# A hybrid decoder block on one core: the later modulation rows in half blocks, and the next chunk's squares one per step

## The chip, the cores and the metric

The kernel runs on one core of one Trainium2 chip. The metric is the device time of one execution in microseconds (us). Before the change it is 2672.51 us, the median of 3 runs (2671.59 to 2675.07). PE is the matmul engine, PEld its weight load, DVE the vector engine, ACT the scalar engine, POOL the GpSimd engine, and SP the engine whose queue issues every DMA of this kernel.

## The reference

The input is a residual stream of 2048 positions by 1024 channels, a condition vector c, and the weights of one decoder layer, all float32.

```
mod = silu(c) @ w_ada + b_ada                # 6 x 1024: sh1, sc1, g1, sh2, sc2, g2
h = rms_norm(x, norm1_g) * (1 + sc1) + sh1
proj = h @ w_in                              # gq gk gv gr glr | aq ak av
y = concat(gla_group(...), dilated_attention_group(...))
x = x + g1 * (y @ w_out)
h = rms_norm(x, norm2_g) * (1 + sc2) + sh2
u = causal_depthwise_conv(h @ w_up, conv_w, conv_b)
out = x + g2 * ((silu(u_gate) * u_val) @ w_down)
```

The modulation vector `mod` has 48 columns of 128 values here. Columns 0 to 15 (sh1, sc1) are wanted before the first projection. Columns 16 to 47 (g1, sh2, sc2, g2), the later modulation, are wanted only when the projections of all chunks are through and the output projection begins.

## The kernel before, in words

**Tiling.** Positions are worked in four chunks of 512 (`T`), channels in blocks of 128 partitions. A float32 product is made of three matmuls in fp32r (`mm3`, L288 to L290): high weights with high input, and the two cross terms. So each block of weights of 512 KB is loaded (`wraw`, 2 slots), rounded on ACT (`whi`, L226, 3 slots) and its remainder taken on DVE (`wlo`, L227, 3 slots), and the matmuls wait for both. `weights` asks for blocks two ahead of their use, in the order of `plan`.

**Stages.** `run` first makes sh1 and sc1 and the normalised input of chunk 0. Then come the projections of the four chunks (`proj`, 26 steps each, a generator that yields after each step), the mixers (`mix`: gated linear attention, then four pairs of attention heads), and per chunk `outproj` and `ffn`. Generators are woven together: `beside` and `along` advance one generator by so many steps for so many steps of the other. The first 27 steps of the projections run alone, the rest beside `mix(0)`, and each later mixer beside the feed-forward part of the chunk before.

**What sets the order.** The program text only gives each instruction a priority. A scheduler at build time puts the instructions of each engine in a fixed list, by priority and by what it believes to be ready, and gives out the slots of tagged tiles. On the chip each engine works through its list in order, and so does SP with the DMAs: an instruction that waits holds up all that stands behind it in its list. The build alone tells the order, and it is shown below with line numbers of the kernel it belongs to.

**The later modulation.** For column b, `ada(b)` loads a 128x1024 row block of `w_ada` (512 KB) into a tile `wada`, yields, and then multiplies it by the condition and sums along the row in one DVE instruction (L330, the product; a second tiny instruction reads the sum), adds the bias (L331), and for sc2 makes the gain `G2` (L335). The 32 later columns share one slot (tag `v4`, also used by the attention's `v4` tile), so the load of column b+1 waits for the product of column b. The generator of the 32 columns is advanced 32 steps for each 46 steps of the projections. The first of these loads (b = 16) waits for a product near the end of the start (`gate_ins`).

**The next chunk's statistics.** `norm_stats(src(c))` loads the eight 128x512 blocks of the chunk's input (256 KB each, tile `sq`, 3 slots), squares each on ACT into another `sq` tile (L360), and sums them on DVE into `acc` (tile `rstd`, 2 slots; L363 copies the first, L365 adds the others). One matmul with `ones` (L367) averages over channels, and Ln and Exp (L369, L370) give the factor. `ahead(proj(c - 1), 10, c)` calls it in one piece after ten steps of the projection before. The blocks are loaded again later for the normalised input (`begin`, through `norm_mod1`, L380 to L384).

Of the kernel before, what the change touches and what calls it, by code (L numbers as in the profile page):

```python
# [19 lines left out]
P = 128  # L20
T = 512
NCH = 4
KD = 8
# [86 lines left out]


def along(a, na, b, nb):

    acc = 0.0
    done = object()
    for _ in b:
        acc += na / nb
        while acc >= 1.0:
            acc -= 1.0
            if next(a, done) is done:  # L120
                acc = -1e9
        yield
    for _ in a:
        pass


def chain(*gs):
    for g in gs:
        yield from g


class K:
# [181 lines left out]

        self.tc.add_manual_dep(inst.ins, self.gate_ins.ins.name, mybir.DependencyInfo(mybir.DependencyClass.Sync, mybir.DependencyReason.DATA))

    def ada(self, b, raws=None):

        nc = self.nc
        if raws is None:  # L320
            raws = [self.at.tile([P, 1024], F32, name="wada", tag="v4", bufs=1)]
        n = 1024 // len(raws)
        for i, raw in enumerate(raws):
            ld = nc.sync.dma_start(raw, self.A["w_ada"][b][:, i * n:(i + 1) * n])
            if b == 16:
                self.after(ld)
        yield
        m = self.mod[:, b:b + 1]
        for i, raw in enumerate(raws):
            self.last = nc.vector.tensor_tensor_reduce(raw, raw, self.cond[:, i * n:(i + 1) * n], 0.5, m if i else 0.0, ALU.mult, ALU.add, m)  # L330
        nc.vector.tensor_tensor(m, m, self.ba[:, b:b + 1], op=ALU.add)  # L331
        for j, G, g in ((1, self.G1, self.n1), (4, self.G2, self.n2)):
            if b // KD == j:
                k = b % KD
                nc.vector.scalar_tensor_tensor(G[:, k:k + 1], m, 1.0, g[:, k:k + 1], op0=ALU.add, op1=ALU.mult)  # L335


    def load_x(self, c):
# [14 lines left out]

    def norm_stats(self, src):

        nc = self.nc
        acc = None
        for k in range(KD):
            sq = self.tmp.tile([P, T], F32, name="sq", bufs=3)
            nc.scalar.activation(sq, src(k), AF.Square)  # L360
            if acc is None:
                acc = self.tmp.tile([P, T], F32, name="rstd", bufs=2)
                nc.vector.tensor_copy(acc, sq)  # L363
            else:
                nc.vector.tensor_tensor(acc, acc, sq, op=ALU.add)  # L365
# [575 lines left out]
    def run(self):  # L941
        self.ada_setup()
        self.scratch()
        self.x1, self.h2, self.tail = {}, {}, ()
        xs = self.load_x(0)
        rstd = {0: self.norm_stats(lambda k: xs[k])}
        h0, ws, done = [], {}, {b: self.pg() for b in FIRST}
        spare = self.at.tile([P, 2048], F32R, name="w0", tag="kt", bufs=2)
        ring = self.at.tile([P, 2048], F32, name="ring", tag="kt", bufs=2)
        for k in range(KD):  # L950
            big = [self.at.tile([P, 1024], F32, name="wada", tag="big", bufs=4)]
            pair = [self.gp.tile([P, T], F32, name="wada", tag=t) for t in ("ghi", "glo")] if k < 5 else [ring[:, k % 2 * 1024:k % 2 * 1024 + 1024]]
            gs = [self.ada(KD + k, big), self.ada(k, pair)]
            for g in gs:
                next(g)
            if k < len(FIRST):
                b = FIRST[k]
                ws[b] = self.wblock(self.A["w_ch"][b], KD, P, True, spare if k == 3 else None)
            for g in gs:
                next(g, None)  # L960
            if k == GATE:
                self.gate_ins = self.last
            h0.append(self.norm_mod1(xs[k], k, rstd[0], self.G1, self.mod[:, 0:8]))
        for b in FIRST:
# [12 lines left out]

        self.wleft, self.wready, self.wpos = list(self.plan()), [], 0
        hs = [h0]

        def begin(c):
            hs.append(self.norm_mod(src(c), rstd[c], self.G1, self.mod[:, 0:8]))

        def proj(c):
            yield from self.proj(c, hs.pop(), (lambda: begin(c + 1)) if c < 3 else None, () if c else done)

        def ahead(g, n, c):

# [12 lines left out]
        for _ in chain(self.outproj(3), self.ffn(3)):  # L1001
            pass
# [61 lines left out]
```

## Time and profile before

| | us |
|---|---|
| median of 3 runs (lowest, highest) | 2672.51 (2671.59, 2675.07) |
| profiled execution: its time, its span | 2676.88, 2675.1 |
| PE busy | 2595.0 (97%) |
| PE weight load busy | 2122.1 (79%) |
| DVE busy | 1891.1 (71%) |
| ACT busy | 1273.2 (48%) |
| POOL busy | 512.1 (19%) |
| mean granted PE clock | 0.989 of full speed |

The span runs from the first to the last instruction of the program. The busy time of PE includes overlap of pipelined matmuls, so what is left of the span is a rough measure of its idle time. DMA moved 405 MB at a mean of 151 GB/s. Times inside the profile are counted from the start of the span. A row of a timeline gives start, duration, engine, line, operation, tiles and count, and in brackets the idle time of the engine before it and what ended that idle time. A row of a wait list gives who waited for whom, the total in us, how often, and the longest.

### The profile page before, as it was taken

The page shows a single profiled execution, that of the slowest core. Times are in us where ns is not written, and L with a number is a line of the kernel's source. Part 1 is how long each engine was busy: PE and PEld are TensorE (multiplying, and loading weights), DVE is VectorE, ACT ScalarE, POOL GpSimd, SP SyncE. Part 2 cuts the span into 40 slices and gives each one's busy share as a digit, 9 for nine tenths or more (in the row PEclk, how much of TensorE's full clock was granted, in tenths as well). Part 3 has the DMA queues.
Part 4 walks back from the last instruction along what each step waited for, and adds up shares of the span by engine and source line. Part 5 has one row for each costly group of instructions (what it writes and reads, how often), then busy time and mean ns, then how long its engine had stood idle before and what let it go on. Part 6 is the DMA issues. An engine that isn't in the chain of part 4 may idle for free.

```text
span 2675.1 us, 46823 instructions
## 1 busy us (share of the span) xinstructions
PE 2595.0 (97%) x18152; PEld 2122.1 (79%) x18152; DVE 1891.1 (71%) x3756; ACT 1273.2 (48%) x2607; POOL 512.1 (19%) x308
## 2 busy tenths in 40 slices
PE   5988999999989999999999999999999999999999
PEld 3777878888768888888788788878888888788887
DVE  8676784665676866777887777778777766666665
ACT  3445556656645455443545444445455443433332
POOL 1142451212221311101231111022211110111110
PEclk9999999999989999999999999999999999999999
DMA  7868455554552244447434444643344445323222
GB/s 276 295 212 276 160 173 170 186 188 150 173 175 95 93 126 133 124 125 241 135 100 135 133 133 129 197 156 122 104 141 138 140 132 180 131 95 101 97 95 95
DMA packets 192127, 405.09 MB, mean 151 GB/s; under 512 B 19473, under 2 KB 70434, under 8 KB 190626
## 3 DMA queue, kind: packets, MB, share of 16 engines
q1 hardware_dynamic: 191906, 402.11, 46.0%
q8 instruction: 143, 2.34, 0.4%
q14 instruction: 78, 0.64, 0.1%
HBM read 339.12 MB, written 62.91 MB: 150 GB/s over the span
## 4 chain that ended last, share of the span: by engine, by line
PE 77%; DVE 5%; ACT 3%; DMA 2%; issue 1%; POOL 0%; SPq 0%; DVEq 0%; ACTq 0%; POOLq 0%
PE psg L288 22%; PE psg L289 22%; PE psg L290 22%; PE psa L719 2%; PE psa L699 2%; PE psa L821 2%; PE psa L557 1%; DVE wlo L227 1%; ACT whi L226 1%; PE psa L816 1%; PE psa L735 1%; ACT big L709 1%; PE psa L627 0%; PE psa L628 0%; DMA sq<-y 0%
## 5 line engine op out<-in xcount | busy, mean ns | idle before, releaser
L288 PE MATMUL psg<-hhi,whi 128*128 128x512 f32 x2040 | 808.7, 399 | 15.6 <-ACT hhi L382 9.0
L289 PE MATMUL psg<-hlo,whi 128*128 128x512 f32 x2040 | 805.6, 395 | 6.4 <-DVE hlo L384 5.0
L290 PE MATMUL psg<-hhi,wlo 128*128 128x512 f32 x2040 | 803.9, 395 | 0.0
L226 ACT CAST whi<-wraw 128x1024 fp32r<-128x1024 f32 (+1 forms) x391 | 409.6, 1049 | 402.5 <-PE psg L289 307.5
L227 DVE TENSOR_TENSOR wlo<-wraw,whi 128x1024 fp32r<-128x1024 f32 (+1 forms) x300 | 386.1, 1287 | 150.2 <-ACT whi L226 141.4
L227 POOL TENSOR_TENSOR wlo<-wraw,whi 128x1024 fp32r<-128x1024 f32 x91 | 223.7, 2459 | 1340.8 <-ACT whi L226 1138.9
L288 PEld LDWEIGHTS psg<-hhi,whi 128*128 128x128 f32 x2040 | 386.2, 190 | 104.8 <-ACT hhi L382 12.3
L289 PEld LDWEIGHTS psg<-hlo,whi 128*128 128x128 f32 x2040 | 386.4, 189 | 90.3 <-DVE hlo L384 9.8
L290 PEld LDWEIGHTS psg<-hhi,wlo 128*128 128x128 f32 x2040 | 386.5, 189 | 82.3 <-issue 2.0
L288 PE MATMUL psg<-ghi,whi 128*128 128x512 f32 x704 | 280.1, 398 | 0.0
L289 PE MATMUL psg<-glo,whi 128*128 128x512 f32 x704 | 277.1, 394 | 0.0
L290 PE MATMUL psg<-ghi,wlo 128*128 128x512 f32 x704 | 276.3, 392 | 0.0
L933 DVE SCALAR_TENSOR_TENSOR x<-psg,mod,x 128x512 f32<-128x512 f32 x192 | 142.7, 747 | 124.4 <-PE psg L290 120.2
L889 DVE SCALAR_TENSOR_TENSOR y<-psg,conv_w_sb,y 128x511 f32<-128x511 f32 x176 | 130.9, 744 | 88.2 <-ACT y L888 87.9
L288 PE MATMUL psg<-whi,hhi 128*128 128x512 f32 (+2 forms) x512 | 177.5, 353 | 10.5 <-DVE stg L461 7.0
L289 PE MATMUL psg<-wlo,hhi 128*128 128x512 f32 (+2 forms) x512 | 178.7, 349 | 7.2 <-DVE wlo L227 7.2
L290 PE MATMUL psg<-whi,hlo 128*128 128x512 f32 (+2 forms) x512 | 177.3, 349 | 0.0
L288 PEld LDWEIGHTS psg<-ghi,whi 128*128 128x128 f32 x704 | 132.5, 188 | 32.2 <-issue 4.5
L290 PEld LDWEIGHTS psg<-ghi,wlo 128*128 128x128 f32 x704 | 132.5, 188 | 28.4 <-issue 1.0
L289 PEld LDWEIGHTS psg<-glo,whi 128*128 128x128 f32 x704 | 132.7, 188 | 28.1 <-issue 2.1
L709 ACT ACTIVATE big<-big,nm 128x256 f32<-128x256 f32 (+1 forms) x256 | 122.4, 479 | 47.1 <-DVE nm L724 47.1
L581 POOL TENSOR_TENSOR pt<-kt,pt 128x512 f32<-128x512 f32 x56 | 92.4, 1650 | 264.2 <-ACT pt L578 186.5
(199 smaller groups left out, 3617.7 us busy)
## 6 DMA issues: line engine op xcount, KB each, us to landing
wraw<-in_w_up_dram SPq DMA_DIRECT2D x176, 512.0 KB, 3.3
wraw<-in_w_down_dram SPq DMA_DIRECT2D x88, 512.0 KB, 3.3
wraw<-in_w_ch_dram SPq DMA_DIRECT2D x48, 512.0 KB, 4.2
wada<-in_w_ada_dram SPq DMA_DIRECT2D x40, 512.0 KB, 5.0
v<-v SPq DMA_DIRECT2D x68, 256.0 KB, 5.1
wraw<-in_w_tokw_dram SPq DMA_DIRECT2D x32, 512.0 KB, 3.9
wraw<-in_w_out_dram SPq DMA_DIRECT2D x32, 512.0 KB, 4.0
sq<-in_xT_dram SPq DMA_DIRECT2D x48, 256.0 KB, 3.9
```

The costliest lines, as they stand in the source:

```text
L226: nc.scalar.copy(hi[:, :n], raw[:, :n])
L227: (nc.gpsimd if pool else nc.vector).tensor_tensor(lo[:, :n], raw[:, :n], hi[:, :n].bitcast(F32), op=ALU.subtract)
L288: nc.tensor.matmul(ps, wh, hh, start=first and k == 0, stop=False, skip_group_check=shared)
L289: nc.tensor.matmul(ps, wh, hl, start=False, stop=False, skip_group_check=shared)
L290: nc.tensor.matmul(ps, wl, hh, start=False, stop=k == n - 1, skip_group_check=shared)
L581: nc.gpsimd.tensor_tensor(kh, gk, df, op=ALU.mult)
L699: nc.tensor.matmul(at(i, hh, z), q[H[hh], i * P:(i + 1) * P], key(H[hh], i, z), start=True, stop=True, skip_group_check=True)
L709: nc.scalar.activation(t[:, lo:hi], t[:, lo:hi], AF.Exp, bias=nm[:, hh, g, i:i + 1], scale=2.0 ** -(h + 1), accum_out=dn[:, hh, g, i:i + 1])
L719: nc.tensor.transpose(ps[:n, i * P:(i + 1) * P], part(S[hh], i), self.C("id"))
L821: nc.tensor.matmul(out, lhsT, rhs, start=first[hh], stop=False, skip_group_check=True)
L889: nc.vector.scalar_tensor_tensor(y[:, 1:], ps[:, :T - 1], self.cw[:, 1, b:b + 1], y[:, 1:], op0=ALU.mult, op1=ALU.add)
L933: nc.vector.scalar_tensor_tensor(x1, ps, self.mod[:, 40 + cb:41 + cb], x1, op0=ALU.mult, op1=ALU.add)
```

## The change

- The later modulation is loaded and multiplied in half blocks: 64 loads of 128x512 (256 KB) and 64 products, in a slot of their own (tag `th`, one slot, otherwise used by the feed-forward part only). A column's second product adds to the sum of its first. The load is traced one step ahead of its product, so the load of a half block waits for the product of the half block before.
- The generator of the 64 half blocks is advanced 64 steps for each 98 steps of the projections, of which there are 104 (before: 32 steps for each 46).
- The statistics of the next chunk are a generator too (`stats`): one load, one square and one addition per step, the load a step ahead; ten steps are spread over the first 16 steps of the projection before. The square is written over its own input, so a block holds one `sq` slot and not two.

```diff
-    def ada(self, b, raws=None):
+    def ada(self, b, raws):
...
+    def ada_late(self):
+
+        nc = self.nc
+        for i in (2, 4, 3, 5):
+            for b in range(8 * i, 8 * i + KD):
+                m = self.mod[:, b:b + 1]
+                for j in range(2):
+                    cols = slice(j * T, (j + 1) * T)
+                    raw = self.up.tile([P, T], F32, name="wada", tag="th", bufs=1)
+                    ld = nc.sync.dma_start(raw, self.A["w_ada"][b][:, cols])
+                    if b == 16 and not j:
+                        self.after(ld)
+                    yield
+                    nc.vector.tensor_tensor_reduce(raw, raw, self.cond[:, cols], 0.5, m if j else 0.0, ALU.mult, ALU.add, m)
+                self.ada_end(b)
...
+    def square(self, acc, x, sq=None):
+
+        nc = self.nc
+        if sq is None:
             sq = self.tmp.tile([P, T], F32, name="sq", bufs=3)
...
+        nc.scalar.activation(sq, x, AF.Square)
+        if acc is None:
+            acc = self.tmp.tile([P, T], F32, name="rstd", bufs=2)
+            nc.vector.tensor_copy(acc, sq)
+        else:
+            nc.vector.tensor_tensor(acc, acc, sq, op=ALU.add)
+        return acc
...
-        def ahead(g, n, c):
-
-            for i, _ in enumerate(g):
-                if i == n:
-                    rstd[c] = self.norm_stats(src(c))
+        def stats(c):
+
+            acc = None
+            x = src(c)(0)
+            for k in range(KD):
                 yield
-
-        gemm = along(chain(*(self.ada(8 * i + k) for i in (2, 4, 3, 5) for k in range(KD))), 32, chain(ahead(proj(0), 10, 1), ahead(proj(1), 10, 2), ahead(proj(2), 10, 3), proj(3)), 46)
+                nx = src(c)(k + 1) if k + 1 < KD else None
+                acc = self.square(acc, x, x)
+                x = nx
+            yield
+            rstd[c] = self.norm_end(acc)
+            yield
+
+        def ahead(c):
+
+            return along(stats(c), 10, proj(c - 1), 16)
+
+        gemm = along(self.ada_late(), 64, chain(ahead(1), ahead(2), ahead(3), proj(3)), 98)
```

`ada_end` holds the bias and gain instructions of `ada` unchanged, and `norm_end` the matmul, Ln and Exp of `norm_stats`. The rows below are the order in which the build puts the instructions: line, operation, output and inputs with tile numbers, size. The line numbers of the changed kernel are its own: L351 is the late product (L330 before), L347 its load, L332 and L336 bias and gain, L383 the square, L386 and L388 copy and addition, L999 the load of an input block, L464 the copy of a finished projection out of PSUM (L437 before), L447 the scaling of a query or key (L420 before), L367 and L369 the two DVE steps of its Newton iteration (L350 and L352 before).

**First place: the start of the late products on DVE.** `wada_496` is the first later block, `wlo_511` (before) and `wlo_517` (now) the remainder of the same first block of `w_av0` weights that the first matmuls after the start wait for.

```order
L330 ISA wada_496,mod_109<-wada_496,cond_93 128x1024
L330 ISA mod_109 128x1
L331 TENSOR_TENSOR mod_109<-mod_109,b_ada_sb_99 128x1
L363 COPY rstd_865<-sq_861 128x512
L227 TENSOR_TENSOR wlo_511<-wraw_508,whi_510 128x1088
L330 ISA wada_503,mod_109<-wada_503,cond_93 128x1024
```

Now:

```order
L386 COPY rstd_509<-sq_496 128x512
L351 ISA wada_498,mod_109<-wada_498,cond_93 128x512
L351 ISA mod_109 128x1
L388 TENSOR_TENSOR rstd_509<-rstd_509,sq_506 128x512
L388 TENSOR_TENSOR rstd_509<-rstd_509,sq_589 128x512
L351 ISA wada_512,mod_109<-wada_512,cond_93,mod_109 128x512
L351 ISA mod_109 128x1
L227 TENSOR_TENSOR wlo_517<-wraw_514,whi_516 128x1088
```

Ahead of the first weights' remainder stand two half products with a load between them, where one whole product stood, and three steps of the statistics where one stood.

On ACT at the same place, `whi` is the rounded first block and `stg_490` the copy that empties the first PSUM bank:

```order
L360 ACTIVATE sq_861<-sq_862 128x512
L226 CAST whi_510<-wraw_508 128x1088
L437 ACTIVATE stg_490<-psg_210 128x512
L360 ACTIVATE sq_867<-sq_868 128x512
L226 CAST whi_516<-wraw_514 128x1088
```

Now:

```order
L383 ACTIVATE sq_496<-sq_496 128x512
L383 ACTIVATE sq_506<-sq_506 128x512
L383 ACTIVATE sq_589<-sq_589 128x512
L226 CAST whi_516<-wraw_514 128x1088
L383 ACTIVATE sq_680<-sq_680 128x512
L464 ACTIVATE stg_490<-psg_210 128x512
```

Four squares stand ahead of the copy where one stood; the fourth, of `sq_680`, needs the slot of `sq_496`, which the first copy on DVE sets free.

**Second place: DVE in the last key blocks of chunk 0.** `stg_1331` (before) and `stg_1309` (now) are the same scaled key block, which ACT waits for (`o16`, L430 before).

```order
L330 ISA wada_1756,mod_109<-wada_1756,cond_93 128x1024
L330 ISA mod_109 128x1
L350 SCALAR_TENSOR_TENSOR nwt_1339<-psa_1334,eps_103,sq_1325 128x512
L331 TENSOR_TENSOR mod_109<-mod_109,b_ada_sb_99 128x1
L352 SCALAR_TENSOR_TENSOR sq_1325<-nwt_1339,sq_1325 128x512
L330 ISA wada_1790,mod_109<-wada_1790,cond_93 128x1024
L330 ISA mod_109 128x1
L420 SCALAR_TENSOR_TENSOR stg_1331<-stg_1332,kgs_473,sq_1325 128x512
```

Now:

```order
L351 ISA wada_2661,mod_109<-wada_2661,cond_93 128x512
L351 ISA mod_109 128x1
L367 SCALAR_TENSOR_TENSOR nwt_1317<-psa_1312,eps_103,sq_1303 128x512
L369 SCALAR_TENSOR_TENSOR sq_1303<-nwt_1317,sq_1303 128x512
L351 ISA wada_2723,mod_109<-wada_2723,cond_93,mod_109 128x512
L351 ISA mod_109 128x1
L447 SCALAR_TENSOR_TENSOR stg_1309<-stg_1310,kgs_473,sq_1303 128x512
```

The two products around the Newton steps keep their places and are of half the width.

**Third place: DVE in the query blocks of chunk 1**, where before all later products are done. `wlo_2481` and `wlo_2561` (before) are the same weights as `wlo_2472` and `wlo_2509` (now).

```order
L227 TENSOR_TENSOR wlo_2481<-wraw_2478,whi_2480 128x1024
L352 SCALAR_TENSOR_TENSOR sq_2202<-nwt_2217,sq_2202 128x512
L420 SCALAR_TENSOR_TENSOR stg_2208<-stg_2209,qgs_471,sq_2202 128x512
L227 TENSOR_TENSOR wlo_2561<-wraw_2558,whi_2560 128x1024
L566 COPY_PREDICATED kt_1792<-masks_sb_460,psa_2332 128x128
```

Now:

```order
L227 TENSOR_TENSOR wlo_2472<-wraw_2469,whi_2471 128x1024
L332 TENSOR_TENSOR mod_109<-mod_109,b_ada_sb_99 128x1
L369 SCALAR_TENSOR_TENSOR sq_2189<-nwt_2204,sq_2189 128x512
L351 ISA wada_4847,mod_109<-wada_4847,cond_93 128x512
L351 ISA mod_109 128x1
L447 SCALAR_TENSOR_TENSOR stg_2195<-stg_2196,qgs_471,sq_2189 128x512
L227 TENSOR_TENSOR wlo_2509<-wraw_2506,whi_2508 128x1024
L351 ISA wada_5031,mod_109<-wada_5031,cond_93,mod_109 128x512
```

Here a half product now stands about every third instruction. In the whole list the last late product stands, before, ahead of the 31st weights' remainder of DVE, and now between the 42nd and the 43rd, which is in the last key blocks of chunk 1. On PE, the last 9968 of 14394 matmuls, which begin in the feed-forward part of chunk 0, stand in the same order in both kernels.

More of the change, by code (lines that the diff above doesn't have):

```diff
@@ L315, in after @@
         self.tc.add_manual_dep(inst.ins, self.gate_ins.ins.name, mybir.DependencyInfo(mybir.DependencyClass.Sync, mybir.DependencyReason.DATA))
-    def ada(self, b, raws=None):
+    def ada(self, b, raws):
         nc = self.nc
-        if raws is None:
-            raws = [self.at.tile([P, 1024], F32, name="wada", tag="v4", bufs=1)]
         n = 1024 // len(raws)
@@ L324, in ada @@
             ld = nc.sync.dma_start(raw, self.A["w_ada"][b][:, i * n:(i + 1) * n])
-            if b == 16:
-                self.after(ld)
         yield
@@ L330, in ada, with ada_end @@
             self.last = nc.vector.tensor_tensor_reduce(raw, raw, self.cond[:, i * n:(i + 1) * n], 0.5, m if i else 0.0, ALU.mult, ALU.add, m)
+        self.ada_end(b)
+    def ada_end(self, b):
+        nc = self.nc
+        m = self.mod[:, b:b + 1]
         nc.vector.tensor_tensor(m, m, self.ba[:, b:b + 1], op=ALU.add)
@@ L335, in ada @@
                 nc.vector.scalar_tensor_tensor(G[:, k:k + 1], m, 1.0, g[:, k:k + 1], op0=ALU.add, op1=ALU.mult)
+    def ada_late(self):
+        nc = self.nc
+        for i in (2, 4, 3, 5):
+            for b in range(8 * i, 8 * i + KD):
+                m = self.mod[:, b:b + 1]
+                for j in range(2):
[6 more added lines that the diff above has]
+                    nc.vector.tensor_tensor_reduce(raw, raw, self.cond[:, cols], 0.5, m if j else 0.0, ALU.mult, ALU.add, m)
+                self.ada_end(b)
     def load_x(self, c):
@@ L354, in norm_stats, with norm_end @@
     def norm_stats(self, src):
-        nc = self.nc
         acc = None
         for k in range(KD):
-            sq = self.tmp.tile([P, T], F32, name="sq", bufs=3)
[L360 to L365, printed above, removed]
+            acc = self.square(acc, src(k))
+        return self.norm_end(acc)
+    def square(self, acc, x, sq=None):
+        nc = self.nc
+        if sq is None:
+            sq = self.tmp.tile([P, T], F32, name="sq", bufs=3)
+        nc.scalar.activation(sq, x, AF.Square)
[5 more added lines that the diff above has]
+        return acc
+    def norm_end(self, acc):
+        nc = self.nc
         ms = self.pa()
```

## The prediction

> **What bounds the kernel now.** I read the page first, then busy time by stage, then what PE waited for in the stages that the change touches, then the timelines around those waits. The page's shares and chain:
>
> ```profile
> PE 2595.0 (97%) x18152; PEld 2122.1 (79%) x18152; DVE 1891.1 (71%) x3756; ACT 1273.2 (48%) x2607; POOL 512.1 (19%) x308
> PE 77%; DVE 5%; ACT 3%; DMA 2%; issue 1%; POOL 0%; SPq 0%; DVEq 0%; ACTq 0%; POOLq 0%
> ```
>
> PE is the bound. The change touches no matmul, so it can only give back or add idle time of PE and the slow clock behind it. By the order, the last 9968 matmuls stand as before; they carry no term. What remains is the stretch of the later products (60 to 266 us), the stretch into which they now reach (266 to 360), and the rest. Busy time by stretch (PE, PEld, DVE, ACT, POOL, then granted PE clock, DMA share, GB/s):
>
> ```profile
> 60.00:266.00 206.00, 186.20 (x1111) 154.78 (x1110) 139.79 (x207) 100.55 (x164) 49.76 (x38) 0.95 0.78 263
> 266.00:360.00 94.00, 88.94 (x830) 72.68 (x832) 70.91 (x100) 56.08 (x109) 49.64 (x34) 0.98 0.46 151
> 180.00:200.00 20.00, 15.02 (x137) 11.36 (x138) 17.32 (x25) 11.48 (x21) 12.34 (x10) 0.76 0.64 211
> 200.00:220.00 20.00, 16.11 (x125) 12.91 (x124) 20.00 (x28) 9.59 (x16) 10.54 (x9) 0.90 0.74 244
> 220.00:240.00 20.00, 17.61 (x88) 15.36 (x87) 10.15 (x17) 8.87 (x13) 0.00 (x0) 0.91 0.92 327
> ```
>
> In the first stretch PE idles 19.8 us and the clock costs (1 - 0.95) x 206 = 10 us more: 30 us are the most that this stretch can return. What PE waited for there, then from 260 to 420:
>
> ```profile
> PE psg L289 <- DVE wlo L227: 7.2, 4, 4.8
> PE psa L411 <- ACT sqr L405: 4.6, 1, 4.6
> PE psg L288 <- DVE stg L461: 3.9, 1, 3.9
> PE psg L288 <- ACT stg L464: 2.4, 1, 2.4
> ...
> PE psa L412 <- POOL sqr L406: 3.0, 2, 1.9
> PE psg L288 <- DVE stg L461: 2.7, 1, 2.7
> ```
>
> In the stretch 220 to 240, PE waits once, 2.4 us, and the clock stands at 0.91: 0.09 x 20 = 1.8 us lost beside the wait. So each wait of over 2 us is charged with 1.8 us of slow clock.
>
> The Trainium skill (TensorE: Matmul & The Clock Gate, section HAM oscillation) has the clock drop only after gaps above some 3.4 us. Here it stands at 0.91 about a wait of 2.4 us, so I go by the row; by the page the sum below would be 1.8 us less.
>
> The later products themselves, from 58 to 266 us, then the loads of the statistics' 256 KB blocks from 360 to 415, where little else is loaded, and the half products that the start already has:
>
> ```profile
> L330 DVE CUSTOM_DVE_ANT_0 wada<-wada,cond x32: 1211/1226/2151, 58.6 to 265.4; 128x1024 f32<-128x1024 f32 x32
>   DMA wada<-in_w_ada_dram: 26.0, 19
> DMA to landing us min/median/max: 3.4/4.2/7.1
> ...
> DMA to landing us min/median/max: 2.5/2.8/4.0
> ...
> L330 DVE CUSTOM_DVE_ANT_0 wada<-wada,cond 128x512 f32<-128x512 f32 x5 | 3.4, 683 | 0.0
> L330 DVE CUSTOM_DVE_ANT_0 wada<-wada,cond,mod 128x512 f32<-128x512 f32 x5 | 3.7, 746 | 0.0
> ```
>
> A whole product takes 1.23 us and its load 3.4 us at best; DVE stood 26.0 us before 19 of them. A half takes 0.72 us, with its sum's read 0.80, and its load 2.5 us at best.
>
> **The change part by part.**
>
> *Pace.* From the chain of waits, two remainders in the stretch that the late products newly reach:
>
> ```profile
> 338.73 1.23 DVE wlo L227
> 356.10 1.35 DVE wlo L227
> ```
>
> One slot makes a chain: product, load, product. Before, a link is 1.3 + 4.2 = 5.5 us, and 31 links make 171 us of the 206.8 between the first and the last product, so the chain alone did not set the pace. Now I estimate the half load at 4.2 - (3.4 - 2.5) = 3.3 us, a link at 4.1, and 63 links at 258 us: the last half product at 317 us if nothing else held it. The order puts it behind the 42nd block of weights, which DVE treated at 349 us before (between the two rows above). So there are some 30 us of room, unevenly spread.
>
> The Trainium skill (DMA: Bandwidth & Descriptors, Rules for kernel authors) advises large transfers, and its section Anatomy of one DMA gives 2.0 us plus the bytes at 436 GB/s. That speaks against the change: 64 x 2.6 us against 32 x 3.2 us, 64 us more load time in the chain. The trace's least values, 2.5 and 3.4 us, say 51. Its sum would change by nothing, as the room stands in both.
>
> *Start of the late products: +2.6 us and a slow clock.* The timelines of DVE, ACT, PE:
>
> ```profile
> 58.62 1.23 DVE L330 CUSTOM_DVE_ANT_0 wada<-wada,cond 128x1024 f32<-128x1024 f32 x1 [0.16 <-DMA wada<-in_w_ada_dram]
> 59.97 0.43 DVE L363 COPY rstd<-sq 128x512 f32<-128x512 f32 x1
> 60.96 1.29 DVE L227 TENSOR_TENSOR wlo<-wraw,whi 128x1088 fp32r<-128x1088 f32 x1 [0.56 <-ACT whi L226]
> 63.30 1.23 DVE L330 CUSTOM_DVE_ANT_0 wada<-wada,cond 128x1024 f32<-128x1024 f32 x1 [1.05 <-DMA wada<-in_w_ada_dram]
> 60.83 0.59 ACT L437 ACTIVATE stg<-psg 128x512 f32<-128x512 f32 x1
> 61.47 0.39 PE L288 MATMUL psg<-whi,hhi 128*128 128x272 f32 x1 [0.81 <-ACT stg L437]
> 62.30 0.39 PE L289 MATMUL psg<-wlo,hhi 128*128 128x272 f32 x1 [0.44 <-DVE wlo L227]
> ```
>
> PE already waits here for ACT's copy (L437) and then for the first remainder (`wlo`). Now a second half product stands ahead of that remainder, and its load can go only when the first is done: 58.6 plus a copy of 0.4 and 0.8 is 59.8, a load of 2.8 gives 62.6, the product 63.4, the remainder 64.7 instead of 62.25. That is +2.5 us for PE. On ACT the copy stands behind the square of `sq_680`, whose load waits for the first copy on DVE (59.1): landed 61.9, squared 62.5, copied 63.1, inside the same delay. Bounds: 0, if the half block lands as soon as the whole did, and +5, if the load takes its 4.2 us and more. I take +2.6 and one slow clock, +1.8: +4.4.
>
> *The wait at 111.9: -4.8 us and a slow clock.*
>
> ```profile
> 98.89 1.39 DVE L330 CUSTOM_DVE_ANT_0 wada<-wada,cond 128x1024 f32<-128x1024 f32 x1 [2.10 <-DMA wada<-in_w_ada_dram]
> 104.14 1.23 DVE L330 CUSTOM_DVE_ANT_0 wada<-wada,cond 128x1024 f32<-128x1024 f32 x1 [2.47 <-DMA wada<-in_w_ada_dram]
> 108.93 1.76 DVE L330 CUSTOM_DVE_ANT_0 wada<-wada,cond 128x1024 f32<-128x1024 f32 x1 [0.66 <-DMA wada<-in_w_ada_dram]
> 111.90 0.79 PE L289 MATMUL psg<-wlo,hhi 128*128 128x512 f32 x1 [4.76 <-DVE wlo L227]
> ```
>
> The eighth remainder stood behind these products and their loads; the links are 5.3 and 4.8 us. Four half products stand in their place, each link some 1.4 us shorter (0.5 of product, 0.9 of load), and the additions of the statistics are through earlier: 5.6 us off a wait of 4.8. Its slow clock goes too. -6.6; bounds -6.6 and -2 (loads that queue).
>
> *The wait at 183.2: -2.3 us and a slow clock.*
>
> ```profile
> 172.79 2.15 DVE L330 CUSTOM_DVE_ANT_0 wada<-wada,cond 128x1024 f32<-128x1024 f32 x1 [1.49 <-DMA wada<-in_w_ada_dram]
> 178.44 1.22 DVE L330 CUSTOM_DVE_ANT_0 wada<-wada,cond 128x1024 f32<-128x1024 f32 x1 [0.73 <-DMA wada<-in_w_ada_dram]
> 179.59 0.75 DVE L420 SCALAR_TENSOR_TENSOR stg<-stg,kgs,sq 128x512 f32<-128x512 f32 x1
> 180.37 1.07 ACT L430 COPY o<-stg 128x512 f32<-128x512 f32 x1 [5.23 <-DVE stg L420]
> 183.16 0.50 PE L411 MATMUL psa<-sqr,blk 128*128 128x512 f32 x1 [4.63 <-ACT sqr L405]
> ```
>
> PE waits for ACT, ACT for a scaled key block of DVE, and DVE stood for two loads of `wada`. The same two products, halved, stand there now (second place of the order): 2 x 1.1 = 2.3 us sooner. The wait halves, and of the two slow clocks in 180 to 200 (0.24 x 20 = 4.8 us) one goes: -4.1. Bounds 0 (ACT is then held by POOL or PE instead) and -8.
>
> *The waits at 196.7 and 207.7 (1.5 and 3.9 us).* DVE is busy all of 200 to 220, so its work is what PE waits for, and three products of it shrink by 0.5 us each: -1.5. Bounds 0 and -9 with both clocks.
>
> *The wait at 233.6 (2.4 us).* ACT empties a bank there only after squares whose loads were late. The new order has four squares ahead of that copy, and the fourth's load waits behind a half product on SP. I take 0; bounds -4.2 and +3.
>
> *The new stretch, 266 to 360.* How matmuls follow each other on PE, from its timeline at a stretch without waits:
>
> ```profile
> 54.81 0.39 PE L290 MATMUL psg<-hhi,wlo 128*128 128x512 f32 x1
> 55.04 0.39 PE L288 MATMUL psg<-hhi,whi 128*128 128x512 f32 x1
> ```
>
> 22 half products move in: 22 x 0.80 = 17.6 us on DVE, which idles 94 - 70.9 = 23.1 us. If each also stands for its load as before (26.0 / 31 = 0.84 us), that is 18.5 more, 36.1 in all, 13 too many. The cover is the ring of three weight slots: PE waited for no remainder from 260 to 420, and two blocks of 24 matmuls at 0.23 us are 11 us in hand. So some 2 us come through; I take +1.5, bounds 0 and +13.
>
> *SP.* The issue of the load that took the shared slot next (`v4`, number left out):
>
> ```profile
> 266.68 0.33 SPq L754 DMA_DIRECT2D v<-v  x1
> ```
>
> 32 more issues of 0.33 us are 10.6 us on a queue that has them in 300 us; a weight load behind a half load waits for a product, as before. The slot is no longer shared with `v4`; that load was issued at 266.7, as soon as the products ended, and nobody waits for it there: 0.
>
> *Sum.* 4.4 - 6.6 - 4.1 - 1.5 + 0 + 1.5 = -6.3. The profiled execution took 2676.88 us (span 2675.1), which is 4.4 us above the median of 2672.51; I carry the difference to the median: 2666.2.
>
> **The rivals.**
>
> *DVE becomes the bound from 266 to 360 (slower).* For: half products every third instruction, and DVE stops in order. It decides when a load costs DVE over (23.1 + 11 - 17.6) / 22 = 0.75 us each; at 1.4 us the overrun is 14.3, with two slow clocks 18: 18 - 7.8 from the other terms gives +10, 2682.7. Against: DMA is busy 0.46 there, against 0.78, and blocks of that size then land in 2.8 us.
>
> *It evens out.* What is won at 111.9 only makes up for the start, ACT at 183 waits for POOL's Newton step anyway, and the new stretch costs 2: within 2 us, 2672.
>
> *DVE leads throughout.* Half products let DVE run ahead by some 1.4 us a link; then all the waits from 111 to 236 go, 17.5 us and five slow clocks, 26.5, less the start's 4.4: 2650.4. For: 30 us are lost there. Against: three of five waits are ACT's, or those of a DVE that is busy throughout.
>
> *The change does not spread as far as it says:* it shows in the order already, products end in chunk 1, and the sum uses that.
>
> **How the numbers follow.** A change of 0.2%, 5.3 us, is about what a measurement of this kernel can tell. Forecast 0.41, between 2660 and 2670; even 0.26; DVE the bound 0.20; DVE leads 0.13. Faster takes the leading case and 0.35 of the forecast's 0.41: 0.48; even, and the forecast's rest less some of either tail: 0.30; slower, the bound and a little of the even case: 0.22. The range leaves out half of the outer cases: 2655 to 2682.
>
> **What would show it.** Right: a PE wait of 3 to 4 us near 62 to 65 us; none near 112; one of 2 us near 180; products of 0.7 us each some 4 us apart, the last near 340; the DVE waits for `wada` at 35 to 45 us in all. Wrong: PE waits for `wlo` or Newton steps between 290 and 370, or a start that costs over 6 us; or none of it, with idle time as before.

## The result and the profile after

The changed kernel takes 2705.67 us (median of 4, 2705.2 to 2708.64) against 2673.79 us for the kernel before (4 runs, 2671.59 to 2675.53): the ratio is 1.0122, with a 95% interval of 1.0107 to 1.0137. It is 32 us slower; the forecast was 2666.2, and 2682 was the upper end of the range. The profiled span grew from 2675.1 to 2703.5 us, by 28.4.

Page of the changed kernel: busy time, and the chain that ended last, by engine and by line:

```profile
PE 2601.6 (96%) x18152; PEld 2125.7 (79%) x18152; DVE 1893.2 (70%) x3820; ACT 1274.8 (47%) x2607; POOL 511.5 (19%) x308
...
PE 81%; DMA 7%; DVE 7%; ACT 2%; issue 2%; POOL 0%; SPq 0%; DVEq 0%; ACTq 0%; POOLq 0%
PE psg L288 24%; PE psg L289 23%; PE psg L290 23%; DMA wada<-in_w_ada_dram 5%; PE psa L726 2%; PE psa L746 2%; PE psa L848 2%; DVE wlo L227 1%; PE psa L584 1%; DVE wada L351 1%; DMA sq<-in_xT_dram 1%; PE psa L762 1%; DVE hlo L411 1%; PE psa L843 1%; ACT whi L226 0%
```

The work is the same: DVE's total moved by 2 us. What is new is in the chain: DMA rose from 2 to 7 per cent, and the loads of `wada` alone hold 5 per cent of the span.

Where the time went can be read off PE. The 9792 matmuls of the weights (those into `psg`) come in the changed kernel in the order of the kernel before but for 98, in the other kernels of the table but for 71 to 235, so the start of the n-th one in two traces gives the lag. Worked out from the traces of one profiled execution each, in us (the labels are those of the experiments below):

```
n-th matmul    start   lag against the kernel before
into psg       before  after    e1    e2    e3    e4    e6    e8    e9   e10
 144             68.3   +4.8  +0.8  +3.1  +0.3  +5.2   0.0  +0.7  +4.7  -1.1
 360            123.6   +3.7  +0.9  -1.4  -0.5  +2.7  -2.6  +2.9  -0.4  +0.3
 936            271.3   +5.8   0.0  -4.2  -5.0  -6.8  -5.4  +1.8  -8.8  +1.4
1440            413.4  +26.7 +19.8  +2.7  +1.4  -0.6  +1.0 +27.3  +1.5  +4.9
2600            706.5  +24.8 +18.8  +0.8 +13.2  -2.5  -1.0 +49.4  -0.4  +4.9
3600            992.6  +29.7 +21.9  +2.9 +17.9  +1.9  +3.5 +51.3  +4.2 +10.8
9791           2670.9  +28.2 +17.9  +1.5 +16.7  +2.0  +3.9 +50.7  +0.9  +9.6
```

The changed kernel lost 4.8 us at the start, gained one by 124, lost two by 271, then 20.9 us between 271 and 413, and 5 more between 706 and 993. After that nothing much happens. The lags are of single executions. Those of the kernel before alone spread from 2669.8 to 2681.94 us (two executions of all, at granted clocks of 0.65 and 0.56, are left out of the ratios). The trace of e1 is its fastest execution, 2694.75 us. So 2 or 3 us in one column prove little.

Busy time of the changed kernel by stretch, in the columns of the prediction, and then the second stretch of the kernel before over the same 154 us:

```profile
60.00:266.00 206.00, 181.72 (x1030) 151.21 (x1029) 128.25 (x209) 96.04 (x156) 50.74 (x37) 0.94 0.72 232
266.00:420.00 154.00, 133.51 (x1259) 106.26 (x1258) 120.89 (x202) 82.82 (x151) 62.93 (x44) 0.92 0.55 177
```

```profile
266.00:420.00 154.00, 146.26 (x1330) 119.81 (x1332) 114.46 (x161) 86.05 (x166) 64.76 (x43) 0.98 0.52 172
```

In the second stretch PE is busy 12.8 us less and its clock fell from 0.98 to 0.92, while DVE has only 6 us more to do. The late products of the changed kernel, their loads and what DVE waited for, from 57 to 420 us:

```profile
L351 DVE CUSTOM_DVE_ANT_0 wada<-wada,cond x32: 677/692/1780, 59.3 to 376.3; 128x512 f32<-128x512 f32 x32
L351 DVE CUSTOM_DVE_ANT_0 wada<-wada,cond,mod x32: 737/752/1329, 63.5 to 381.1; 128x512 f32<-128x512 f32 x32
  DMA wada<-in_w_ada_dram: 77.7, 46
DMA to landing us min/median/max: 2.5/3.3/6.8
```

DVE stood 77.7 us before 46 half products, against 26.0 us before 19 whole ones. In its list of waits from 266 to 420 this is the first row; before, the same row was 3.1 us:

```profile
DVE wada L351 <- DMA wada<-in_w_ada_dram: 27.7, 17, 3.7
```

What PE waited for in the changed kernel, 60 to 266 and then 266 to 420:

```profile
PE psg L289 <- DVE wlo L227: 6.8, 4, 3.3
PE psg L288 <- ACT stg L491: 6.1, 2, 3.3
PE psa L439 <- POOL sqr L433: 4.7, 3, 3.7
PE psa L584 <- DVE pt L607: 2.6, 1, 2.6
...
PE psa L439 <- POOL sqr L433: 8.3, 5, 3.4
PE psg L288 <- DVE stg L488: 5.3, 1, 5.3
PE psa L654 <- DVE state L664: 1.8, 1, 1.8
```

All rows of the second stretch add up to 20.4 us, against 7.9 in the kernel before, and the slower clock costs (0.98 - 0.92) x 154 = 9 us more: some 22 us, about the 20.9 that were lost. None of these rows names `wada`. The way from the load to PE goes through DVE's order, as at the wait of 3.36 us at 361. Timelines of DVE, POOL and PE:

```profile
353.77 0.69 DVE L351 CUSTOM_DVE_ANT_0 wada<-wada,cond 128x512 f32<-128x512 f32 x1 [3.13 <-DMA wada<-in_w_ada_dram]
355.11 0.69 DVE L603 TENSOR_TENSOR pt<-kt 128x512 f32<-128x512 f32 x1
355.72 0.74 DVE L367 SCALAR_TENSOR_TENSOR nwt<-psa,eps,sq 128x512 f32<-128x512 f32 x1
357.30 1.15 DVE L351 CUSTOM_DVE_ANT_0 wada<-wada,cond,mod 128x512 f32<-128x512 f32 x1 [0.83 <-DMA wada<-in_w_ada_dram]
...
356.61 1.29 POOL L368 TENSOR_TENSOR nwt<-nwt,sq 128x512 f32<-128x512 f32 x1 [7.78 <-DVE nwt L367]
357.86 1.71 POOL L608 TENSOR_TENSOR pt<-kt,pt 128x512 f32<-128x512 f32 x1
359.53 1.71 POOL L433 TENSOR_TENSOR sqr<-sq,sqr 128x512 fp32r<-128x512 f32 x1
...
361.29 0.80 PE L439 MATMUL psa<-sqr,blk 128*128 128x512 f32 x1 [3.36 <-POOL sqr L433]
```

DVE stands 3.13 us for a half block. The Newton step behind it is late, POOL has stood 7.78 us for that step, and works it off ahead of the split square that PE wants. PE's wait list puts the wait down to POOL. From 266 to 420 POOL stood three times as long for that step as before (changed kernel, then before):

```profile
POOL nwt L368 <- DVE nwt L367: 34.3, 6, 16.3
POOL nwt L351 <- DVE nwt L350: 11.5, 5, 6.9
```

SP stood for the slot too in that stretch, 61 us, and held up what was behind it in its list. Little came through that way: DVE waited there for no other load, ACT 7.3 us for loads (6.6 before), and PE for no block of weights.

### The profile page after: what moved, and what is told of

The parts are those of the page before. It is cut to its first block, busy times and chain, and to the rows that moved or that the text cites. A ratio compares the mean times of both kernels' runs of the same rounds, so it can differ in the third digit from the quotient of the medians.

```text
span 2703.5 us, 46978 instructions
## 1 busy us (share of the span) xinstructions
PE 2601.6 (96%) x18152; PEld 2125.7 (79%) x18152; DVE 1893.2 (70%) x3820; ACT 1274.8 (47%) x2607; POOL 511.5 (19%) x308
## 4 chain that ended last, share of the span: by engine, by line
PE 81%; DMA 7%; DVE 7%; ACT 2%; issue 2%; POOL 0%; SPq 0%; DVEq 0%; ACTq 0%; POOLq 0%
PE psg L288 24%; PE psg L289 23%; PE psg L290 23%; DMA wada<-in_w_ada_dram 5%; PE psa L726 2%; PE psa L746 2%; PE psa L848 2%; DVE wlo L227 1%; PE psa L584 1%; DVE wada L351 1%; DMA sq<-in_xT_dram 1%; PE psa L762 1%; DVE hlo L411 1%; PE psa L843 1%; ACT whi L226 0%
## 5 line engine op out<-in xcount | busy, mean ns | idle before, releaser
L288 PE MATMUL psg<-whi,hhi 128*128 128x512 f32 (+2 forms) x512 | 178.0, 354 | 14.6 <-DVE stg L488 6.6
```

The costliest lines, as they stand in the source:

```text
L288: nc.tensor.matmul(ps, wh, hh, start=first and k == 0, stop=False, skip_group_check=shared)
```

## The experiments

Theory S: the single slot makes a chain in which DVE stands for nearly every load, and what is queued behind it is late. Theory P: not the waits but the half products themselves, now in chunk 1, are too much for DVE. Theory T: the statistics, one square per step, are what is late.

**e1, half blocks with the old statistics.**

```diff
...
-            return along(stats(c), 10, proj(c - 1), 16)
...
+            for i, _ in enumerate(g):
+                if i == n:
+                    rstd[c] = self.norm_stats(src(c))
                 yield
...
```

> Half blocks at the new pace, but the next chunk's statistics in one piece as in the kernel before. Theory S (one slot: DVE stands for nearly every half load, 77.7 us in 46 waits, and what queues behind it is late): the 18.9 us lost between 266 and 420 stay, only the 4.8 us of the start can go: 2697 to 2706. Theory P (pace: half products fall into chunk 1, where DVE has no room, whatever they wait for): the same. Theory T (the spread statistics are what is late): under 2685.

Measured 2700.78 us (ratio 1.0099, 1.0081 to 1.0118), DVE's waits 70.3 us. In the range of S and P; T falls. The start is back to +0.8, and 19.8 us are lost between 271 and 413 all the same.

**e2, whole blocks with the new statistics.** The kernel before with the generator `stats`.

> Whole blocks at the old pace in the shared slot, as in the kernel before, but the statistics one square per step. Theories S and P: within 8 us of the kernel before, 2670 to 2682, with the start's few us if the squares ahead of the first copy cause them. Theory T: 2690 to 2705.

Measured 2676.82 us (1.0006, 0.9997 to 1.0016): no change that can be told. T falls from this side too. The lag column shows more: 3.1 us lost at the start, a lead of 4.2 at 271, and none left at 413. DVE's waits for the 32 whole loads are 35.0 us here, not 26.0. So the like with like is 35.0 against the 77.7 us of the changed kernel (new statistics), and 26.0 against the 70.3 of e1 (old statistics).

**e3, two slots, one of them shared with `v4`.**

```diff
-                    raw = self.up.tile([P, T], F32, name="wada", tag="th", bufs=1)
+                    raw = self.up.tile([P, T], F32, name="wada", tag="th", bufs=1) if j else self.at.tile([P, 1024], F32, name="wada", tag="v4", bufs=1)[:, :T]
```

> The changed kernel with first halves in the slot shared with v4 and second halves in the slot th, so that each load has a whole product's time of room. Theory S: DVE's waits for wada fall from 77.7 us to under 25, the stretch 266 to 420 loses under 6 us, and what is left is the start and the stretch 780 to 830: 2678 to 2690. Theory P: the waits fall, the time does not: over 2695. Theory T: over 2695 too.

Measured 2695.87 us (1.0078, 1.0063 to 1.0094): S is wrong, and P and T (over 2695) are met by under 1 us. DVE's waits for `wada`, which were to fall under 25 us with two slots, are still 48.1. The reason is in the late products of this kernel from 500 to 720 us:

```profile
L351 DVE CUSTOM_DVE_ANT_0 wada<-wada,cond x11: 692/693/1749, 513.7 to 694.5; 128x512 f32<-128x512 f32 x11
L351 DVE CUSTOM_DVE_ANT_0 wada<-wada,cond,mod x11: 737/752/1610, 515.3 to 695.3; 128x512 f32<-128x512 f32 x11
  DMA wada<-in_w_ada_dram: 21.4, 11
```

The attention took the shared slot after 42 half products, and the other 22 stand behind it, with 21.4 us of waiting. The loss moved with them: level at 413 (+1.4), 13.2 us behind at 706. So the run doesn't test two slots. It shows that the loss is where the late products and their waits stand, and both S and P say that.

**e4, no late loads.** The products read the condition vector itself.

```diff
-                    ld = nc.sync.dma_start(raw, self.A["w_ada"][b][:, cols])
...
-                    nc.vector.tensor_tensor_reduce(raw, raw, self.cond[:, cols], ...)
+                    pr = nc.vector.tensor_tensor_reduce(raw, self.cond[:, cols], self.cond[:, cols], ...)
...
```

> The changed kernel without the 64 late loads: the half products read a vector that is there already, so the modulation values are not the reference's. DVE keeps its 64 x 0.8 us of work and waits for no load; DMA and SP have 64 transfers less. Theory S: 2668 to 2685. Theory P: over 2692. Theory T: over 2692.

Measured 2676.34 us (1.0003, 0.9994 to 1.0012). As S says; but the build moved all products ahead of the 16th block of weights (the last starts at 152 us), so none stood in chunk 1, and P isn't tested. That is what e9 is for.

**e5 and e6, one slot and two.** Both load the bias into `mod`, which frees the 192 bytes that a second slot needs.

```diff
-        self.mod = self.const.tile([P, 48], F32, name="mod")
+        self.mod = self.ba
...
-        nc.vector.tensor_tensor(m, m, self.ba[:, b:b + 1], op=ALU.add)
```

and e6 alone, at both uses of the tag:

```diff
-                    raw = self.up.tile([P, T], F32, name="wada", tag="th", bufs=1)
+                    raw = self.up.tile([P, T], F32, name="wada", tag="th", bufs=2)
...
-                    th = self.up.tile([P, T], F32, name="th", bufs=1)
+                    th = self.up.tile([P, T], F32, name="th", bufs=2)
```

> The changed kernel with the bias b_ada loaded into mod itself, as the value that a column's first product starts from, so that the additions of 0.15 us and 192 bytes of a partition fall away. It is the control for the next run; the late products still reach to the 42nd block of weights. Both theories: like the changed kernel, 2698 to 2709.

> The same with two slots th, which the 192 bytes make room for; nothing else is edited. The order then has the last late product ahead of the 30th block of weights, not the 43rd. Theory S (the waits behind a single slot): DVE's waits for wada fall from 78 us to under 35, no late product stands in chunk 1's key blocks, 2672 to 2685. Theory P (half products cost DVE in place of whole ones: 64 x 0.8 against 32 x 1.3 us, and their number is the loss): over 2693.

Measured on one chip: 2702.69 us with one slot (1.0099, 1.0082 to 1.0116), as both theories said, and 2680.33 with two (1.0017, 1.0008 to 1.0027), as S said. The second slot is worth 22 us. The products and DVE's waits with one slot, then with two:

```profile
L350 DVE CUSTOM_DVE_ANT_0 wada<-wada,cond,b_ada_sb x64: 737/752/1810, 59.4 to 377.8; 128x512 f32<-128x512 f32 x64
  DMA wada<-in_w_ada_dram: 79.6, 46
...
L350 DVE CUSTOM_DVE_ANT_0 wada<-wada,cond,b_ada_sb x64: 734/750/1652, 58.6 to 251.9; 128x512 f32<-128x512 f32 x64
  DMA wada<-in_w_ada_dram: 38.8, 27
```

The last of the same 64 products starts at 252 us in place of 378, and DVE waits 38.8 us in place of 79.6; S had said under 35. The number of the products is not the loss. But with two slots none of them stands in chunk 1 either, so the waits and the place are not told apart here; e9 does that.

**e7, two slots with the old pace and the old statistics.**

> Two slots as in the run before, with the old pace (64 half blocks per 46 steps) and the statistics in one piece. Theory S: the start's 4.8 us go too, and the products stand no later than in the kernel before: 2664 to 2676. Theory P: over 2690.

Measured 2685.76 us (1.0039, 1.0024 to 1.0054): wrong, it is 5 us slower than e6. From 230 to 300 us PE waited for ACT (`stg` L490, `sqr` L431) 3.4 and 3.3 us in e7, 1.3 and 0.9 in e6, 4.5 us less. The spread squares may be what helps e6 here, but the pace was undone in the same run, so the two aren't told apart.

**e8, quarter blocks in one slot.**

```diff
-                for j in range(2):
-                    cols = slice(j * T, (j + 1) * T)
-                    raw = self.up.tile([P, T], F32, name="wada", tag="th", bufs=1)
+                for j in range(4):
+                    cols = slice(j * 256, (j + 1) * 256)
+                    raw = self.up.tile([P, T], F32, name="wada", tag="th", bufs=1)[:, :256]
...
-        gemm = along(self.ada_late(), 64, ...
+        gemm = along(self.ada_late(), 128, ...
```

> The changed kernel with quarter blocks (128 loads of 128x256, one slot of the same tag). The suspected cost doubled: theory S has 128 links with a wait of 1.2 us or more each, 150 us and more of DVE waiting spread over two chunks, of which some two thirds come through to PE: 2725 to 2765. Theory P (DVE's work in chunk 1, not its waits): the work grows by 64 x 0.35 us = 22 us, 2700 to 2718.

Measured 2726.8 us (1.0192, 1.0177 to 1.0208), in the range of S. DVE's waits from 57 to 700, and the loads:

```profile
  DMA wada<-in_w_ada_dram: 154.3, 96
DMA to landing us min/median/max: 2.2/2.7/5.9
```

Half the size makes about twice the waiting each time: 35.0 (e2), 77.7 and 154.3 us for 32, 64 and 128 products, all with the new statistics. The load of a quarter still takes 2.7 us, and there are four.

**e9, the products at their places, without loads.** As e4, but each product is tied to the block of weights that it follows in the changed kernel (`LATE`).

```diff
+                    while len(self.los) < LATE[0]:
+                        yield
+                    n = LATE.pop(0)
+                    ...
+                        self.tc.add_manual_dep(pr.ins, self.los[n - 1].ins.name, ...)
```

> The 64 half products on a vector that is there already (the 64 late loads left out, so the modulation values are not the reference's), but each made to follow the block of weights that it follows in the changed kernel, so that they reach to the 42nd block as there. DVE has the same work at the same places and waits for no load. Theory S (the waits behind the single slot): the stretch 266 to 420 loses no more than in the run with products on resident data that ran early (about 6 us), 2670 to 2685. Theory P (DVE has no room for 25 products in chunk 1): over 2695.

Measured 2679.52 us (1.0015, 1.0005 to 1.0024). Busy time by stretch:

```profile
60.00:266.00 206.00, 190.90 (x1208) 160.40 (x1209) 145.66 (x225) 107.96 (x171) 52.68 (x39) 0.96 0.57 190
266.00:420.00 154.00, 141.71 (x1232) 115.96 (x1231) 127.88 (x204) 80.55 (x157) 63.76 (x42) 0.94 0.49 163
```

DVE did 127.9 us of work from 266 to 420, more than in the changed kernel (120.9), with products up to the 42nd block. PE lost 10.3 us between 271 and 413 (from -8.8 to +1.5), where the changed kernel lost 20.9, and e2, e3, e4 and e6, without late products there, 6.2 to 6.9: some 4 us may be the products' work (S had said about 6 in all). P falls as the cause: there is room for the products, not for their waits. Without the waits 26 of the 32 us are gone. They cost in both stretches: against e9 the changed kernel is 14.6 us behind at 271 and 25.2 at 413. The run also leaves out the traffic and SP's issues; but e6 has both and is 22 us faster than e5, so they are not most of it.

**e10, the kernel before with the bias in `mod`** (the first edit of e5 alone).

> The kernel before with one small edit: b_ada is the value that a column's product starts from, and 48 additions of 0.15 us fall away. Whole blocks, old pace, old statistics. Yet the order of DVE in chunk 0's output projection (about 750 to 830 us) turns into the one of the changed kernel, with a step of the attention and a block of weights ahead of the last additions of the statistics. If that order is what costs 4 to 5 us there: level with before up to 750, and 3 to 5 us behind after 830, 2674 to 2680. If half blocks cost it: 2668 to 2674.

Measured 2683.41 us (1.0027, 1.0017 to 1.0036): slower than either side said, and not level up to 750 (+4.9 there). But between 706 and 993 it loses 5.9 us. Ten kernels with the changed kernel's order at that place were run (the changed one, e1, e3 to e10); nine lost 3.1 to 6.3 us there, e8 1.9. With another order, e2 lost 2.1. What PE waited for from 740 to 860, in e10 and then in the kernel before:

```profile
PE psg L288 <- ACT hhi L856: 4.3, 1, 4.3
PE psa L366 <- DVE rstd L364: 4.1, 1, 4.1
PE psg L288 <- ACT hhi L381: 2.8, 1, 2.8
```

```profile
PE psa L367 <- DVE rstd L365: 2.9, 1, 2.9
PE psg L288 <- ACT hhi L857: 2.7, 1, 2.7
```

Whole blocks in the old slot, and yet the row for `rstd` stands at 4.1 us, as in the changed kernel. The last additions of the statistics there, in DVE's timeline of the kernel after:

```profile
812.12 2.88 DVE L388 TENSOR_TENSOR rstd<-rstd,sq 128x512 f32<-128x512 f32 x1
814.93 0.68 DVE L603 TENSOR_TENSOR pt<-kt 128x512 f32<-128x512 f32 x1
...
817.38 1.68 DVE L227 TENSOR_TENSOR wlo<-wraw,whi 128x1024 fp32r<-128x1024 f32 x1 [0.53 <-ACT whi L226]
...
819.18 0.68 DVE L607 TENSOR_TENSOR pt<-kt,pt 128x512 f32<-128x512 f32 x1
819.78 0.68 DVE L388 TENSOR_TENSOR rstd<-rstd,sq 128x512 f32<-128x512 f32 x1
```

Attention steps (`pt`) stand between the last two additions; in the kernel before, none does. PE's own order differs there as well: in the traces of the changed kernel and of the kernel before, PE's matmuls stand alike only from 867 us of the changed one on, and those from 787 to 867 are partly woven otherwise. So these 5 us come together with another order far from the edit, which a small edit brings too. How much of them the order makes alone isn't settled (see e11).

**e11 and e12, another weave.** `beside(self.mix(1), 68, ..., 94)` in place of 86, in the kernel before and in e6, to get the better order.

> The kernel before with mix(1) woven 68 steps to 94 of the output projection and feed-forward part of chunk 0 (86 before). The order then has the squares' additions of that statistics with nothing of the attention between the last ones. If such an order is worth what the rows at 793 to 801 say (waits of 2.9, 1.3 and 1.2 us and a slow clock of 10 us): 2666 to 2672; else 2672 to 2678.

> Two slots, the spread statistics, and the same weave of 68 to 94. If the 4.5 us that the two-slot run lost from 780 to 830 go: 2672 to 2678; if the order that is left there costs as much: 2678 to 2684.

Both wrong: 2693.31 (1.0066, 1.005 to 1.0082) and 2696.81 (1.008, 1.0066 to 1.0094). Around 790, e11 neither gained nor lost (a lead of 2.1 us at 744, of 2.3 at 847). It loses between 1226 and 1277 us of its trace, where a lead of 6.8 turns into a lag of 19.5: at 94 the last steps of that mixer are left over and run without the feed-forward part beside them (300 matmuls that are not of weights stand together from 1247 to 1269 us, with 10.8 us of waits), and the next output projection starts late; 14.9 are left at the end.

No version was found that beats the kernel before.

## Why the prediction was wrong, point by point

The step that failed is what a half product waits for its load. I took a shorter load for a shorter chain, and 0.84 us of waiting for each half product that the weight slots would hide; the runs show links of 5.1 us, 77.7 us of waiting, and 26 of the 32 us gone when no product waits (e9).

- **The load: right. The link, and the pace with it: wrong.** The half load lands in 3.3 us at the median, as estimated, and the last product was said to be at 317 if nothing else held it. It came at 381. The 63 links take (381.1 - 59.3) / 63 = 5.1 us, not 4.1.
- **Start, +4.4: measured +4.8.** The size was right, the cause only in part. PE's timeline of the changed kernel, here and at the place of the next point:

```profile
63.67 0.39 PE L288 MATMUL psg<-whi,hhi 128*128 128x272 f32 x1 [1.29 <-ACT stg L464]
65.56 0.40 PE L289 MATMUL psg<-wlo,hhi 128*128 128x272 f32 x1 [1.49 <-DVE wlo L227]
...
112.42 0.50 PE L289 MATMUL psg<-wlo,hhi 128*128 128x512 f32 x1 [1.44 <-DVE wlo L227]
120.03 0.50 PE L288 MATMUL psg<-hhi,whi 128*128 128x512 f32 x1 [2.78 <-ACT stg L491]
```

  PE waited for ACT's copy and then for the remainder. In e4 and e9 no product waits for a load, and the start is as late (+5.2, +4.7); four squares stand ahead of ACT's copy there as in the changed kernel. In e3 and e6, with the same statistics but two squares ahead of the copy, it is +0.3 and 0.0. So the squares ahead of the copy, which I had inside the delay of the product, are part of the cause. They don't settle it alone: with three squares there, e8 starts at +0.7 and e5 at +4.9.
- **The wait at 111.9, -6.6: measured -1.1 (4.8 to 3.7).** This step failed first, and it was wrong by its own figures. I counted each of four half products as a link that is 1.4 us shorter, but four have three links between them where three whole ones have two: 3 x 4.1 = 12.3 us against 5.3 + 4.8 = 10.1. The chain gets longer, and I took the difference as a gain. I also took DVE's wait to shrink with the load. The timeline of DVE shows that halves wait like wholes:

```profile
106.89 0.75 DVE L351 CUSTOM_DVE_ANT_0 wada<-wada,cond,mod 128x512 f32<-128x512 f32 x1 [1.57 <-DMA wada<-in_w_ada_dram]
110.53 0.69 DVE L351 CUSTOM_DVE_ANT_0 wada<-wada,cond 128x512 f32<-128x512 f32 x1 [2.02 <-DMA wada<-in_w_ada_dram]
```

  The wait at 112 shrank from 4.76 to 1.44 us, but one of 2.78 us for ACT came at 120. It goes back to the same chain: SP could issue a load of weights only at 112.39, after the remainder that stands behind the product of 110.53 on DVE, and ACT stood for that load ahead of its copies:

```profile
118.45 1.04 ACT L226 CAST whi<-wraw 128x1024 fp32r<-128x1024 f32 x1 [8.63 <-DMA wraw<-in_w_ch_dram]
```

- **The waits from 183 to 234, -5.6 together: measured +2.1 by 271.** DVE waited for more loads, and longer for each. At 182.4 PE waited 3.68 us where 2 were forecast, now for POOL. From 60 to 266 DVE stood 50.0 us for 39 loads, 1.28 each, where it had stood 26.0 us for 32, 0.81 each.
- **The new stretch, +1.5 (0 to +13): measured +20.9 by 413.** This term was mis-sized most. I took 0.84 us of waiting for each half product, the value of whole ones; it was 27.7 / 25 = 1.11, for 25 products and not 22. The rival in which DVE is the bound had named the place and the condition, over 0.75 us each, and still gave only 2682.7, since I let the ring of weights swallow 11 us and took off 7.8 us of gains. But PE's waits there are not for remainders: they are for split squares behind a Newton step on POOL, for the state and for emptied banks, which the ring of weights doesn't cover.
- **A gain before 271 doesn't last.** The sum carried each gain to the end. The five runs that led at 271 by 4.2 to 8.8 us (e2, e3, e4, e6, e9) were between -0.6 and +2.7 at 413. In e9 PE waits near 384 for DVE's step that empties a bank (`stg`), 5.9 us in place of 2.7; in the other four 3.8 to 4.3. PE's wait in e9, and what ACT does ahead of its own part of that step (L497):

```profile
PE psg L293 <- DVE stg L498: 5.9, 1, 5.9
...
381.44 0.63 ACT L393 ACTIVATE sq<-sq 128x512 f32<-128x512 f32 x1 [0.93 <-DMA sq<-in_xT_dram]
382.09 1.28 ACT L497 ACT_TABLE_LOAD   x1
```

  A square of the next chunk's statistics, which in e9 waits for its load, stands ahead there in all five, and all five have the new statistics. In the kernel before, e7 and e10, with the old ones, none does, and PE's wait is 2.6 to 2.7 us. That the square makes the difference is not shown: in e1, with the old ones too but late products, the wait is 4.3. So even without the new waits the -6.3 would not have been seen.
- **The rest, 0: measured +5 at 706 to 993, together with another order there.** I had given no term to anything behind 360 us, but the matmuls that stand as before begin only at 867 in the changed kernel's trace, and I had not looked at DVE's and PE's order ahead of them.
- **What would show it.** The waits for `wada` were to be 35 to 45 us and were 77.7. PE waits for Newton steps between 290 and 370 were among the signs of being wrong; what came were waits for squares that stood behind a Newton step on POOL.
- **The rule of the Trainium skill that spoke against the change** (DMA: Bandwidth & Descriptors, Rules for kernel authors, to prefer large transfers) was set aside since the chain had room. The trace agrees with the rule: waits of 35.0 (e2), 77.7 and 154.3 us with blocks of 512, 256 and 128 KB. The formula that the Trainium skill gives in Anatomy of one DMA is fitted there to transfers issued by GpSimd, and these are issued by SP; the estimate by it, 2.6 and 3.2 us for a load, is near the least durations here, 2.5 and 3.4. It made 64 us more load time in the chain, the least durations 51; DVE's waiting grew by 43 us against e2 and by 52 against the kernel before. That time was in the prediction, and was costed at nothing.

## What to carry to other kernels

With one slot, a load starts only when the product before it is done, so making blocks smaller adds links. Here the least load time fell only from 3.4 to 2.5 to 2.2 us as the block was halved twice, while the loads doubled each time, and DVE's waiting about doubled with them. Find the room for a second slot before making blocks smaller; here 192 bytes were worth 22 us, though not a gain over the kernel before. And price a wait by everything that is queued behind it on an engine that works in order: the engine that PE then waits for is often another one.

## What the runs showed that was not expected

The clock can fall after a short wait. After a single wait of 1.8 us at 321 (the row for the state above), the changed kernel's clock in the next 4 us (in the 14 us behind it is back at 1.00):

```profile
322.00:326.00 4.00, 4.00 (x23) 3.28 (x22) 0.91 (x2) 1.65 (x10) 0.92 (x1) 0.57 0.69 240
```

That is 0.43 x 4 = 1.7 us on top of a wait of 1.8. The Trainium skill (TensorE: Matmul & The Clock Gate, HAM oscillation) gives the rule as no idle gaps above some 3.4 us; here half of that was enough, and the measurement decides. The second surprise is how little it takes to shift the build's order: taking out 48 additions of 0.15 us made the kernel before 8 us slower (e10).
